# Step-size products of a hybrid S5/SSD layer: three-part split operands against full f32 in four column strips

## The chip, the cores and the metric

One core of a Trainium2 chip runs one layer of a streaming encoder in f32. The engines are PE (TensorE, matrix products; its weight loads are listed as PEld), DVE (VectorE), ACT (ScalarE), POOL (GpSimd) and SP (which issues DMAs). The metric is the device time of one execution in microseconds, lower is better. Before the change it was 1020.19 us, the median of three runs (1015.82 to 1021.0).

## The reference, cut to what matters

```python
hn   = rmsnorm(h, norm_w)                       # h = x: (1, 1024, 1024)
proj = hn @ w_in                                # (1024, 5136)
u_s5, z_s5, z_ssd, xBC, dt_raw = split(proj)    # dt_raw: the last 16 columns
...
dt = softplus(dt_raw + dt_bias)                 # step sizes, 16 heads
A  = -exp(A_log)
a_cs = cumsum(dt * A)                           # within chunks of 64 steps
y = ssd_chunked(xs, dt, A, Bm, Cm) + Dh * xs
```

The change concerns dt_raw, the product of the normalised input with the last 16 columns of w_in. The root of the mean square, which the norm divides by, is one number for each of the 1024 time steps, so it can be applied after the product.

## The kernel before, in words

The input is held transposed: eight tiles xt of 128 channels by 1024 steps, loaded by L677 and L686. The large products run in a split form: an operand is rounded to the format fp32r (hi) and the rest kept beside it (lo), and a product is hi x hi + lo x hi + hi x lo, each in one pass of PE (dense_k, L149 to L154; every call is 512 columns wide).

The first stage (L654 to L739) does the following for each of the eight input tiles k: ACT makes hi = norm_w x xt (L704; L679 for the first tile, in halves), DVE makes lo (L705, L680), ACT squares xt (L711) and DVE adds the squares into acc (L712). The weight of the step sizes, wd (128 x 8 x 16), is loaded by L697; wdr holds its hi part in 16 columns and the rest in 16 more (L698, L699). L715 then multiplies, for each tile, both column halves h and both parts i of the input with the 32 columns of wdr, and adds up over the eight tiles in two banks of PSUM, dps. So there are 32 products of 128 x 32 weights with 128 x 512 columns, and rows 0 to 15 and 16 to 31 of the result belong to the two parts of the weight.

Behind the loop, L718 copies the 32 rows of dps to dtR. rsqrt_bcast (L169 to L185) sums acc over the partitions with an f32 product with ones (L176, two calls of 512 columns), and ACT turns it into rstdB, one over the root, on all partitions. dt_scale (L483, on GpSimd) multiplies dtR with rstdB into dtF, and reorders. The first three tiles of u (L721 to L725) need hi and lo of the un-normalised input and are scaled afterwards; everything behind them uses the normalised tiles, for which DVE multiplies xt with rstdB (L729), ACT rounds (L731) and DVE takes the rest (L735).

dt_chain (L487) transposes dtF and adds up its parts with eight small products (L491) with the constant sel, whose rows repeat the 16 x 16 identity eight times; then it computes softplus and the sums over a chunk. It runs after the third tile of u.

In s5_weights stands a product that is used for comparison: L373 multiplies f32 weights of 128 x 32 with 128 columns, for q = 0 to 3 into rows 32q to 32q + 31 of one bank, with tile_position=(0, 32 * q), two of them for each q.

A planner sets the order of the instructions on each engine when the kernel is built: it simulates the engines and takes, of the instructions whose inputs are there in its plan, the one that stands first in the program. On the chip each engine follows that order and waits by semaphores. Where `in_line` is called, an order is written out by hand (L708 and L739). DMAs are all issued from SP, in one queue.

Of the kernel before, what the change touches and what calls it, by code (L numbers as in the profile page):

```python
# [8 lines left out]
F32 = mybir.dt.float32  # L9
# [4 lines left out]
P = 128  # L14
# [40 lines left out]
def hybrid_layer(ctx: ExitStack, tc: tile.TileContext, xT, pT, w_in, w_dt, w_glu, w_out, w_gate, w_ple,  # L55
# [426 lines left out]

    def dt_scale(dtF, raw):  # L483
        G.tensor_tensor(dtF.rearrange("p (k t c) -> p t k c", k=8, t=8), raw.rearrange("p (t k c) -> p t k c", t=8, k=8),
                        rstdB[:32].rearrange("p (t k c) -> p t k c", t=8, k=8), ALU.mult)

    def dt_chain(dtF):  # L487
        with tc.tile_pool(name="pt", bufs=1) as pt:
            tp = psa()
            for k in range(8):  # L490
                T.matmul(tp[:, 16 * k:16 * k + 16], dtF[:, k * P:(k + 1) * P], cs_("sel")[:32], start=True, stop=True)  # L491
            e_ = pt.tile([P, P], F32, tag="e_", name="e_")
            w_ = pt.tile([P, P], F32, tag="w_", name="w_")
            s2 = pt.tile([P, P], F32, tag="s2", name="s2")
            fd = dt2.rearrange("p k h -> p (k h)")
            V.tensor_tensor(dt2, tp[:, :P].rearrange("p (k h) -> p k h", k=8),
                            pr("dtb")[:, None, :].broadcast_to([P, 8, 16]), ALU.add)

            S.activation(e_, fd, AF.Abs)
            S.activation(e_, e_, AF.Exp, scale=-1.0)  # L500
            V.tensor_scalar(w_, e_, 2.0, None, ALU.add)
            V.reciprocal(w_, w_)
            V.tensor_tensor(e_, e_, w_, ALU.mult)
            V.tensor_tensor(s2, e_, e_, ALU.mult)
            V.tensor_scalar(w_, s2, 2.0 / 17, 2.0 / 15, ALU.mult, ALU.add)
            for d in (13, 11, 9, 7, 5, 3, 1):
                V.tensor_tensor(w_, w_, s2, ALU.mult)
                V.tensor_scalar(w_, w_, 2.0 / d, None, ALU.add)
            V.tensor_tensor(w_, w_, e_, ALU.mult)
            V.scalar_tensor_tensor(fd, fd, 0.0, w_, ALU.max, ALU.add)  # L510
            nA = pt.tile([P, 16], F32, tag="nA", name="nA")
            S.activation(nA, pr("alog"), AF.Exp)
            V.tensor_scalar(nA, nA, -1.0, None, ALU.mult)
            a_ = pt.tile([P, 8, 16], F32, tag="a_", name="a_")
            V.tensor_tensor(a_, dt2, nA[:, None, :].broadcast_to([P, 8, 16]), ALU.mult)
            fa = a_.rearrange("p k h -> p (k h)")
            cp = psa()
            rp = psa()
            T.matmul(cp[:, 0:P], cs_("triM"), fa, start=True, stop=True)
            T.matmul(cp[:, P:2 * P], cs_("sup"), fa, start=True, stop=True)  # L520
            T.matmul(cp[:, 2 * P:3 * P], ones, fa, start=True, stop=True)
            T.matmul(rp[:, 0:P], fa, cs_("triM"), start=True, stop=True)
            T.matmul(rp[:, P:2 * P], fa, cs_("tri0"), start=True, stop=True)
            rows = pt.tile([P, 2, P], F32, tag="rows", name="rows")
            V.tensor_copy(csM, cp[:, 0:P])
            S.activation(dtd.rearrange("p k h -> p (k h)"), cp[:, P:2 * P], AF.Exp)
            V.tensor_tensor(dtd, dtd, dt2, ALU.mult)
            S.activation(totE, cp[:, 2 * P:3 * P], AF.Exp)
            V.tensor_copy(rows[:, 0], rp[:, 0:P])
            S.activation(rows[:, 1], rp[:, P:2 * P], AF.Exp)  # L530
            dma(Rd.rearrange("a p c -> p a c"), rows)
# [117 lines left out]
    xhl = []  # L649
    es_t = ExitStack()  # L650
    dpool = es_t.enter_context(tc.tile_pool(name="dpool", bufs=1))
    dtF = dpool.tile([32, NT], F32, tag="dtF", name="dtF")
    pu = es_t.enter_context(tc.tile_pool(name="pu", bufs=2))
    with tc.tile_pool(name="p0", bufs=2) as p0:  # L654
        acc = p0.tile([P, NT], F32, tag="acc", name="acc", bufs=1)
        wd = p0.tile([P, 8, 16], F32, tag="wd", name="wd", bufs=1)
        wdr = p0.tile([P, 8, 32], F32R, tag="wdr", name="wdr", bufs=1)
        wt, xts = [], []
        pu_ps = [[psd(), psd()], [psd(), psd()]]
        dps = [psa(), psa()]  # L660
        pu_ps.append([psa(), psa()])

        zero = p0.tile([P, 512], mybir.dt.bfloat16, tag="zero", name="zero", bufs=1)
        V.memset(zero, 0.0)
        for _ in range(NWARM):
            T.matmul(dps[0], zero[:, 0:P], zero, start=True, stop=True)
        for k in range(KT):
            xt = p0.tile([P, NT], F32, tag="xt", name="xt", bufs=8)
            if k == 0:

                hi, lo = xslot(k, "x")
                raw = wpool.tile([P, NT], F32, tag="wraw", name="wraw")
                whi = wpool.tile([P, NT], F32R, tag="whi", name="whi")
                wlo = wpool.tile([P, NT], F32R, tag="wlo", name="wlo")
                line = []
                for h in range(2):
                    dma(hf(xt, h), hf(xT[k], h))  # L677
                    dma(hf(raw, h), hf(wsrc[0][0], h))
                    line.append(S.activation(hf(hi, h), hf(xt, h), AF.Copy, scale=pr("normw", k)))  # L679
                    V.scalar_tensor_tensor(hf(lo, h), hf(xt, h), pr("normw", k), hf(f(hi), h), ALU.mult, ALU.subtract)  # L680
                    line.append(S.activation(hf(whi, h), hf(raw, h), AF.Copy))
                    V.tensor_tensor(hf(wlo, h), hf(raw, h), hf(f(whi), h), ALU.subtract)
                wt.append((whi, wlo))
                wat[0] = 1
            else:
                dma(xt, xT[k])  # L686
            if k == 2:
                dma(cst_t, cst)
                V.tensor_copy(ones_r, ones)
            if k == 1 or k == 4:  # L690
                wp[0] = wpool if k < 2 else p0
                wfetch(1)
                wt.append(wq.pop(0))
                wp[0] = wpool
            if k == 0:

                dma(wd.rearrange("p k m -> p (k m)"), w_dt)  # L697
                V.tensor_copy(wdr[:, :, 0:16], wd)  # L698
                V.tensor_tensor(wdr[:, :, 16:32], wd, f(wdr)[:, :, 0:16], ALU.subtract)  # L699
            xts.append(xt)  # L700
            if k > 0:
                hi, lo = xslot(k, "x")
                nw = pr("normw", k)
                S.activation(hi, xt, AF.Copy, scale=nw)  # L704
                V.scalar_tensor_tensor(lo, xt, nw, f(hi), ALU.mult, ALU.subtract)  # L705
            xhl.append((hi, lo))
            if k == 0:
                in_line(line + [S.activation(acc, xt, AF.Square)])  # L708
            else:
                sq = p0.tile([P, NT], F32, tag="sq", name="sq")  # L710
                S.activation(sq, xt, AF.Square)  # L711
                V.tensor_tensor(acc, acc, sq, ALU.add)  # L712
            for h in range(2):
                for i in range(2):
                    T.matmul(dps[h][:32], wdr[:, k], hf(xhl[k][i], h), start=(k == 0 and i == 0), stop=(k == 7 and i == 1))  # L715
        dtR = p0.tile([32, NT], F32, tag="dtR", name="dtR", bufs=1)
        for h in range(2):
            S.copy(hf(dtR, h), dps[h][:32])  # L718
        rsqrt_bcast(rstdB, acc, 1.0 / NT)
        dt_scale(dtF, dtR)  # L720
        for k in range(KT):  # L721
            for m in range(2):
                dense_k(pu_ps[m], wt[m], xhl, k, KT, HALVES)
        for k in range(KT):
            dense_k(pu_ps[2], wt[2], xhl, k, KT, HALVES)  # L725

        xhl, line = [], []
        for k in range(KT):
            line.append(V.scalar_tensor_tensor(xts[k], xts[k], pr("normw", k), rstdB, ALU.mult, ALU.mult))  # L729
            hi, lo = xslot(k, "xn")  # L730
            S.activation(hi, xts[k], AF.Copy)  # L731
            xhl.append((hi, lo))
            if k % 2:
                for i in (k - 1, k):
                    line.append(V.tensor_tensor(xhl[i][1], xts[i], f(xhl[i][0]), ALU.subtract))  # L735
            if k == 1:
                us = [pu.tile([P, NT], F32, tag="u", name="u") for _ in range(2)]
                line += [V.tensor_tensor(js(hf(us[0], h)), sj(pu_ps[0][h]), sj(hf(rstdB, h)), ALU.mult) for h in range(2)]
        in_line(line)  # L739
# [266 lines left out]
```

## Time and profile before

| what | value |
|---|---|
| median of three runs | 1020.19 us |
| profiled execution | 1020.48 us |
| its span, first to last instruction | 1018.2 us |
| PE busy | 970.5 us (95%) |
| DVE busy | 612.4 us (60%) |
| ACT busy | 458.4 us (45%) |
| POOL busy | 248.9 us (24%) |
| mean granted clock of PE | 0.980 of full speed |

The profile is of one execution. Busy times count an engine from the start to the end of each instruction. A matmul lasts longer than the distance to the next, since they are pipelined: what one costs is read from the distance between two starts. An f32 product shows as more than one record with its weight load. An entry such as 128*32 128x512 is the weight's rows and columns, and the moving operand.

### The profile page before, as it was taken

Reading aid. Unit: us, or ns where it says so; the run is one execution under the profiler, and the core shown is the slowest. Engines: PE = TensorE matmul, PEld = TensorE weight load, DVE = VectorE, ACT = ScalarE, POOL = GpSimd, SP = SyncE. Lnnn points to the kernel's source line nnn. Section 1 sums busy time; section 2 is a strip of 40 time slices with the busy share of each in tenths; the row PEclk is TensorE's granted clock in tenths of the full one; section 3 lists DMA queues with packets and bytes.
Section 4 is the critical chain, followed back from the end, with each engine's and each line's share of the span. In section 5 each row is a group of like instructions: output and inputs, shape, how many; then the busy total and the mean of one; then the engine's idle time right before and its main releaser. Section 6 shows DMA issues by size and latency. Waiting matters only on the chain. (4 is left out here: it accounts for less than half of the span.)

```text
span 1018.2 us, 13114 instructions
## 1 busy us (share of the span) xinstructions
PE 970.5 (95%) x4992; PEld 812.0 (80%) x4992; DVE 612.4 (60%) x971; ACT 458.4 (45%) x603; POOL 248.9 (24%) x167
## 2 busy tenths in 40 slices
PE   8999999989999999999799989999999989999994
PEld 5778777778888888888678768888887668899994
DVE  7698798936998991000568556687542411544577
ACT  8354142255765434332376353484213731462363
POOL 0000000000000050101033864333323174332454
PEclk9999999998999999999799999999999989999998
DMA  7135778496341228889946744576324650011133
GB/s 293 41 90 163 210 233 262 133 244 174 102 145 63 83 104 249 230 258 192 342 141 214 257 121 139 173 238 206 88 83 128 187 181 30 1 54 56 57 137 123
DMA packets 136270, 158.56 MB, mean 156 GB/s; under 512 B 6288, under 2 KB 108688, under 8 KB 135184
## 3 DMA queue, kind: packets, MB, share of 16 engines
q1 hardware_dynamic: 136208, 157.74, 51.5%
q8 instruction: 39, 0.64, 0.3%
q14 instruction: 23, 0.19, 0.1%
HBM read 118.06 MB, written 39.65 MB: 155 GB/s over the span
## 5 line engine op out<-in xcount | busy, mean ns | idle before, releaser
L133 POOL TENSOR_TENSOR wlo<-wraw,whi 128x1024 fp32r<-128x1024 f32 x52 | 139.5, 2685 | 286.9 <-ACT whi L130 213.6
L130 ACT ACTIVATE whi<-wraw 128x1024 fp32r<-128x1024 f32 x79 | 83.3, 1055 | 260.2 <-PE psd L154 211.9
L154 PE MATMUL psd<-xnlo,whi 128*128 128x512 f32 x592 | 185.5, 393 | 0.2 <-DVE xnlo L735 0.2
L154 PE MATMUL psd<-xnhi,wlo 128*128 128x512 f32 x592 | 185.4, 393 | 0.2 <-DVE wlo L133 0.2
L154 PE MATMUL psd<-xnhi,whi 128*128 128x512 f32 x592 | 184.4, 392 | 0.0
L154 PEld LDWEIGHTS psd<-xnlo,whi 128*128 128x128 f32 x592 | 111.0, 188 | 24.6 <-DVE xnlo L735 1.0
L154 PEld LDWEIGHTS psd<-xnhi,wlo 128*128 128x128 f32 x592 | 110.8, 188 | 24.6 <-issue 1.6
L154 PEld LDWEIGHTS psd<-xnhi,whi 128*128 128x128 f32 x592 | 110.8, 188 | 23.4 <-issue 0.8
L566 DVE SCALAR_TENSOR_TENSOR csB<-csB,csM,cst_t 128x128 f32<-128x128 f32 x128 | 50.3, 466 | 119.5 <-DMA zc<-Zd 108.1
L546 DVE SCALAR_TENSOR_TENSOR cv<-pad,prm_t,cv 128x1024 f32<-128x1024 f32 x48 | 65.6, 1366 | 3.6 <-ACT cv L544 3.3
L154 PE MATMUL psd<-hhi,whi 128*128 128x384 f32 (+1 forms) x192 | 50.7, 318 | 0.5 <-DVE gt L875 0.5
L154 PE MATMUL psd<-hlo,whi 128*128 128x384 f32 (+1 forms) x192 | 50.8, 317 | 0.0
L154 PE MATMUL psd<-hhi,wlo 128*128 128x384 f32 (+1 forms) x192 | 50.7, 317 | 0.0
L154 PE MATMUL psd<-nhi,whi 128*128 128x512 f32 x128 | 41.1, 407 | 6.4 <-ACT whi L130 3.8
L133 DVE TENSOR_TENSOR wlo<-wraw,whi 128x1024 fp32r<-128x1024 f32 x27 | 32.8, 1219 | 23.1 <-PE psd L154 15.8
L849 DVE TENSOR_TENSOR h<-h,psd 128x512 f32<-128x512 f32 x16 | 10.3, 682 | 58.6 <-PE psd L154 58.6
L154 PE MATMUL psd<-yhi,whi 128*128 128x512 f32 x128 | 40.5, 396 | 4.3 <-DVE m L809 4.2
L537 POOL MEMSET pad<- 128x3 f32 x16 | 1.6, 102 | 175.5 <-DMA Cd<-pad 161.3
L154 PE MATMUL psd<-nlo,whi 128*128 128x512 f32 x128 | 41.5, 404 | 0.1
L154 PE MATMUL psd<-ylo,whi 128*128 128x512 f32 x128 | 41.4, 398 | 0.0
L154 PE MATMUL psd<-nhi,wlo 128*128 128x512 f32 x128 | 41.0, 404 | 0.0
L154 PE MATMUL psd<-yhi,wlo 128*128 128x512 f32 x128 | 40.8, 397 | 0.0
(291 smaller groups left out, 1894.3 us busy)
## 6 DMA issues: line engine op xcount, KB each, us to landing
wraw<-in_w_in_dram SPq DMA_DIRECT2D x39, 512.0 KB, 4.3
Cd<-pad SPq DMA_DIRECT2D x16, 512.0 KB, 2.9
Zd<-z SPq DMA_DIRECT2D x16, 512.0 KB, 5.9
ug<-Ud SPq DMA_DIRECT2D x16, 512.0 KB, 4.3
cc<-Cd SPq DMA_DIRECT2D x8, 1024.0 KB, 6.7
csB<-Rd SPq DMA_DIRECT2D x8, 1024.0 KB, 11.6
wraw<-in_w_out_dram SPq DMA_DIRECT2D x16, 512.0 KB, 3.4
wraw<-in_w_gate_dram SPq DMA_DIRECT2D x16, 512.0 KB, 3.4
```

Source lines behind the costliest of these rows:

```text
L130: S.activation(hi, raw, AF.Copy)
L133: E.tensor_tensor(lo, raw, f(hi), ALU.subtract)
L154: T.matmul(p, w[:, c], rhs[k][r][:, x], start=(k == 0 and j == 0), stop=(k == nk - 1 and j == 2))
L537: G.memset(pad[:, 8:11, 0:1], 0.0)
L546: conv_last[0] = V.scalar_tensor_tensor(cv, pad[:, d:d + 8, 1:129], pr("convw", 4 * m + d), cv, ALU.mult, ALU.add)
L566: i_ = V.scalar_tensor_tensor(csB[:, h], csB[:, h], csM[:, 16 * k + h:16 * k + h + 1], cap, ALU.subtract, ALU.min)
L849: V.tensor_tensor(hf(h_t[m], h), hf(h_t[m], h), ps[h], ALU.add)
```

## The change

wdr becomes f32: 128 x 8 x 32, with zeros in 16 of the 32 columns and norm_w x wd in the others. The products read the input tile xt itself instead of its hi and lo, without norm_w, which the weight now holds. They are issued at k = 3 and at k = 7 for four tiles each; tile k - 3 + q goes to rows 32q to 32q + 31 of dps, in the array's column strip q. So each strip adds up two tiles, dps has 128 rows, and dtR and dtF have 128 partitions instead of 32. dt_scale and L491 take 128 rows; sel, whose rows repeat, adds up the four strips.

```diff
     def dt_scale(dtF, raw):
         G.tensor_tensor(dtF.rearrange("p (k t c) -> p t k c", k=8, t=8), raw.rearrange("p (t k c) -> p t k c", t=8, k=8),
-                        rstdB[:32].rearrange("p (t k c) -> p t k c", t=8, k=8), ALU.mult)
+                        rstdB.rearrange("p (t k c) -> p t k c", t=8, k=8), ALU.mult)
...
-                T.matmul(tp[:, 16 * k:16 * k + 16], dtF[:, k * P:(k + 1) * P], cs_("sel")[:32], start=True, stop=True)
+                T.matmul(tp[:, 16 * k:16 * k + 16], dtF[:, k * P:(k + 1) * P], cs_("sel"), start=True, stop=True)
...
-    dtF = dpool.tile([32, NT], F32, tag="dtF", name="dtF")
+    dtF = dpool.tile([P, NT], F32, tag="dtF", name="dtF")
...
-        wdr = p0.tile([P, 8, 32], F32R, tag="wdr", name="wdr", bufs=1)
+        wdr = p0.tile([P, 8, 32], F32, tag="wdr", name="wdr", bufs=1)
...
-                V.tensor_copy(wdr[:, :, 0:16], wd)
-                V.tensor_tensor(wdr[:, :, 16:32], wd, f(wdr)[:, :, 0:16], ALU.subtract)
+                V.memset(wdr, 0.0)
+                V.tensor_tensor(wdr[:, :, 0:16], wd, pr("normw")[:, :, None].broadcast_to([P, 8, 16]), ALU.mult)
...
-            for h in range(2):
-                for i in range(2):
-                    T.matmul(dps[h][:32], wdr[:, k], hf(xhl[k][i], h), start=(k == 0 and i == 0), stop=(k == 7 and i == 1))
-        dtR = p0.tile([32, NT], F32, tag="dtR", name="dtR", bufs=1)
+            if k % 4 == 3:
+
+                for h in range(2):
+                    for q in range(4):
+                        T.matmul(dps[h][32 * q:32 * q + 32], wdr[:, k - 3 + q], hf(xts[k - 3 + q], h),
+                                 start=(k == 3), stop=(k == 7), tile_position=(0, 32 * q))
+        dtR = p0.tile([P, NT], F32, tag="dtR", name="dtR", bufs=1)
         for h in range(2):
-            S.copy(hf(dtR, h), dps[h][:32])
+            S.copy(hf(dtR, h), dps[h])
```

## Rows read from the trace of the kernel before

**Rows 1.** The page, part 1: busy us (share of the span) and instructions of each engine.

```profile
PE 970.5 (95%) x4992; PEld 812.0 (80%) x4992; DVE 612.4 (60%) x971; ACT 458.4 (45%) x603; POOL 248.9 (24%) x167
```

**Rows 2.** Stretch, length; busy us of PE, PEld, DVE, ACT, POOL; clock, DMA, GB/s.

```profile
5.00:10.00 5.00, 3.47 (x11) 1.40 (x10) 3.04 (x6) 3.82 (x6) 0.00 (x0) 1.00 0.99 356
10.00:15.00 5.00, 4.81 (x22) 3.27 (x21) 4.96 (x6) 4.79 (x6) 0.00 (x0) 1.00 1.02 417
...
20.00:25.00 5.00, 5.00 (x24) 3.51 (x23) 5.00 (x5) 4.95 (x6) 0.00 (x0) 1.00 0.31 120
```

**Rows 3.** Timeline of PE, 9 to 13 us: start us, us, engine, line, operation.

```profile
9.15 0.43 PE L715 MATMUL psa<-xhi,wdr 128*32 128x512 f32 x1 [0.20 <-DVE wdr L699]
...
10.10 0.62 PE L715 MATMUL psa<-xhi,wdr 128*32 128x512 f32 x2
...
11.38 0.65 PE L715 MATMUL psa<-xlo,wdr 128*32 128x512 f32 x2 [0.19 <-DVE xlo L705]
11.87 0.62 PE L154 MATMUL psd<-xlo,whi 128*128 128x512 f32 x2
12.33 0.63 PE L154 MATMUL psd<-xhi,wlo 128*128 128x512 f32 x2
```

**Rows 4.** Instructions of line L715: duration ns min/median/max, first and last start.

```profile
L715 PE MATMUL psa<-xhi,wdr x16: 387/396/426, 9.1 to 30.9; 128*32 128x512 f32 x16
```

**Rows 5.** Timeline of PEld (weight loads), 33 to 36 us.

```profile
33.67 0.41 PEld L176 LDWEIGHTS psa<-acc,cst_t 128*128 128x128 f32 x2
34.32 0.19 PEld L176 LDWEIGHTS psa<-acc,cst_t 128*128 128x128 f32 x1 [0.24 <-issue]
34.75 0.19 PEld L176 LDWEIGHTS psa<-acc,cst_t 128*128 128x128 f32 x1 [0.24 <-issue]
35.18 0.19 PEld L154 LDWEIGHTS psd<-xlo,whi 128*128 128x128 f32 x1 [0.24 <-issue]
```

**Rows 6.** Timeline of PE around L373, 109 to 112 us.

```profile
109.96 0.61 PE L154 MATMUL psd<-xnhi,wlo 128*128 128x512 f32 x2
110.50 0.66 PE L373 MATMUL psa<-CA,Bbd 128*32 128x128 f32 x14
111.09 0.73 PE L154 MATMUL psd<-xnhi,whi 128*128 128x512 f32 x2
111.66 0.39 PE L154 MATMUL psd<-xnlo,whi 128*128 128x512 f32 x1
```

**Rows 7.** Timeline of ACT and DVE, 14 and 27 us: one row each.

```profile
14.12 1.16 ACT L704 ACTIVATE xhi<-xt,prm_t 128x1024 fp32r<-128x1024 f32 x1 [0.21 <-DMA xt<-in_xT_dram]
...
27.64 1.22 DVE L712 TENSOR_TENSOR acc<-acc,sq 128x1024 f32<-128x1024 f32 x1
```

**Rows 8.** Timeline of DVE and PE, with line L484's own row between.

```profile
38.98 4.74 DVE L729 SCALAR_TENSOR_TENSOR xt<-xt,prm_t,rstdB 128x1024 f32<-128x1024 f32 x2 [10.12 <-ACT rstdB L185]
...
49.95 2.46 DVE L729 SCALAR_TENSOR_TENSOR xt<-xt,prm_t,rstdB 128x1024 f32<-128x1024 f32 x2
...
L484 POOL TENSOR_TENSOR dtF<-dtR,rstdB x1: 2409/2409/2409, 39.0 to 39.0; 32x1024 f32<-32x1024 f32 x1
...
50.25 1.95 PE L491 MATMUL psa<-cst_t,dtF 32*128 32x16 f32 x16
```

**Rows 9.** Waits, us in total, times, longest: 50 to 60 us, 60 to 230 us.

```profile
PEld psd L154 <- DVE xnlo L735: 0.8, 2, 0.6
...
PE psa L373 <- DVE CA L366: 2.6, 2, 1.3
PE psa L373 <- DVE CA L363: 0.9, 2, 0.6
...
PE psa L407 <- DMA ug<-Ud: 4.1, 1, 4.1
```

**Rows 10.** The page, part 5: line L133 on GpSimd, busy us, mean ns, idle before.

```profile
L133 POOL TENSOR_TENSOR wlo<-wraw,whi 128x1024 fp32r<-128x1024 f32 x52 | 139.5, 2685 | 286.9 <-ACT whi L130 213.6
```

**Rows 11.** Busy time by stretch again, 210 to 240 us.

```profile
210.00:240.00 30.00, 25.45 (x133) 22.14 (x132) 7.42 (x8) 16.21 (x29) 0.27 (x4) 0.89 0.93 224
```

## The prediction, made before the changed kernel was run

> **What bounds the kernel now.** I read the page's busy times first: PE (TensorE's matmuls) is busy 95% of the span, DVE 60% [rows 1]. So time taken from PE is time off the end, wherever PE has work queued. Next the busy times by stretch over the first 40 us, where the edited instructions lie [rows 2]: PE is short of work from 5 to 10 us (3.47 of 5 us), nearly full from 10 us (4.81 of 5), and full in 20 to 25 us, while the loads end soon after 20 us (DMA share 0.31 in 20 to 25 us, so some 1.6 us of it). Then PE's own order there, instruction by instruction [rows 3]: the step-size products of L715 stand between the dense ones of L154, two at a time, as each half of an input tile gets ready. PE's order is fixed when the kernel is built: a planner simulates the engines and issues what its plan holds ready, earlier program lines first. The pairs of L715 (the hi part for both column halves, later the lo part) show this, since the program's own loop would put hi and lo beside each other. Last I read what follows: the squares' sum [rows 5, 7], rstdB and the normalised tiles on DVE [rows 8], and the places where PE later waits for DVE [rows 9].
>
> **What is removed.** 32 products of 128x32 by 128x512 in one pass (16 on the hi part, row shown, 16 on the lo part alike) [rows 4]. In the full stretch two follow each other in 0.46 us (11.87 to 12.33) [rows 3], so each costs 0.23 us of PE although one lasts 0.396, and 32 cost 7.3 us. Not all of it is on the path. The first eight run from 9.15 to about 11.87, when PE has little else: after them it waits for xlo of the second tile, which comes at 11.38 [rows 3]. Without them the four dense products that start at 11.87 could start at 11.38: 0.5 us. The other 24 stand in the full stretch: 24 x 0.23 = 5.5 us. Saved: 6.0 us.
>
> **What is added.** 16 products in f32. How the chip runs f32 with 512 columns is shown by the squares' sum at L176: two calls make four records, whose weight loads start 0.43 us apart (34.32, 34.75, 35.18) [rows 5]. So one f32 product is two passes of 0.43 us, and 16 are 32 passes: 13.8 us if they run one by one. Whether four tiles in four column strips run at once is shown by L373, which has the same stationary shape (128x32, f32), the same four strips and 128 columns. There 14 passes take 0.66 us from first start to last end [rows 6]. A pass of 128 columns by the 0.43 us for 512 is 0.107 us, so 14 in a row would be 1.5 us plus the tail; four strips, of which the fullest has four passes, are 4 x 0.107 = 0.43 us plus a tail of some 0.25. The second fits. The same rows give the price of going in and out: the dense product before starts at 110.18 (second of the two at 109.96), the next would have started at 110.41 and starts at 111.09, and the two there take 0.57 instead of 0.46. That is 0.68 + 0.11 = 0.79 us for 0.43 us of streaming, so 0.36 us for one clump.
>
> One tile's pair (both column halves, two passes each) lies in one strip: 4 x 0.43 = 1.72 us, and 2.07 us with the way in and out. Pairs that stand together share those 2.07 us; pairs with dense products between them pay it each. Two whole groups of four are 4.1 us; eight lone pairs are 16.6.
>
> The TensorE page of the Trainium skill ("TensorE: Matmul & The Clock Gate", Part 3: Packing small matmuls) says that matmuls start and end strictly in program order. By that a strip's second pass would hold back the next strip's first, and L373's passes in its program's order would need about eleven rounds, or 1.2 us plus the tail. The 0.66 us speaks against it; the rule is a rival below.
>
> **How the passes will stand.** The new products read the input tiles themselves, so in the plan a pair is ready when its tile has landed, not when hi and lo are made. The tiles land over the first 21.6 us: the fourth at 14.1 us, for which ACT waits [rows 7], the last by about 21.6 [rows 2]. Between these two lie six loads of one size, four tiles and two of weights: some 1.25 us each, so tiles come 1.25 or, with a weight load between, 2.5 us apart, around the 1.72 us of a pair. So I expect neither one clump for each group nor eight lone pairs. Pairs one and two stand together before 10.4 us, in the gap that the first old products filled, and cost nothing; if that cover is gone they cost 2.07. Of the other six I take three clumps, of one, two and three pairs: 3 x 2.07 = 6.2 us. PE: 6.2 - 6.0 = +0.2 us. The bounds are -3.9 (one clump on the path) and +6.4 (six lone pairs, 12.4 - 6.0).
>
> **What moves with it.** PE gets to L176 at 33.67 [rows 5], but its input acc is ready at 27.64 + 1.22 = 28.86 [rows 7]: rstdB comes 4.8 us later than it could, because PE has a backlog ahead of L176. DVE's chain of the normalised tiles starts from rstdB, at 38.98 after a wait of 10.12 us [rows 8]. With more PE time given to the products, the plan puts fewer dense products ahead of L176, and rstdB can come 0 to 4.8 us earlier; I take half, 2.4 us, since the trace does not show the planner's price of an f32 pass. That is worth something as PE waits for DVE behind it: 0.8 us for xnlo at 50 to 60 us, and 2.6 + 0.9 us for CA at L373 from 60 to 230 us, 4.3 us together [rows 9]. Worth 2.4 us. A later acc cannot come of it: the sums on ACT and DVE are untouched.
>
> **The small edits.** The cast of wd and its remainder become a memset, needing no load, and one product, on DVE, which is busy for 3.04 of 5 us there [rows 2]: 0, and 0.5 us if it had no gap. The copies to dtR keep 512 columns on each partition and only get more partitions: 0, at a place where PE holds the queue ahead of rstdB anyway. dt_scale on GpSimd goes from 32 to 128 partitions with the same 1024 elements each: it takes 2.41 us now [rows 8], and a 128x1024 operation of GpSimd takes 2.69 [rows 10]. So 0 to +0.3 us; I take 0.1, near the row of the same operation. DVE does feel it: its two L729 beside dt_scale take 4.74 us, two others 2.46 [rows 8], and PE would see at most that 0.3. L491 has the weights 128 rows deep instead of 32, with 16 passes in 1.95 us as before [rows 8]: 0. No queue gets a new DMA.
>
> **The sum.** The profiled execution took 1020.48 us (span 1018.2 and 2.3 around it), 0.3 above the median of 1020.19. 1020.5 + 0.2 + 0.1 - 2.4 = 1018.4 us.
>
> **The rivals.**
> A, fours together: the planner holds a group as one clump, as L373's 14 are. PE: between 2.07 and 4.1 on the path, -3.9 to -1.9, say -2.9, and rstdB moves by a little more, -1: 1016.6. For it: [rows 6]. Against it: L373's inputs come at once, from one operation, the tiles do not.
> B, lone pairs (slower): dense products get between all six pairs; it decides as soon as tiles land further apart in the plan than a pair takes there. Each strip then works alone, 12.4 us against 6.0: +6.4, less up to 2.4 from rstdB: 1024.5 to 1027. For it: L715's halves stand apart, with dense work between them [rows 3].
> C, PE waits at L176: the plan overrates the passes, puts so few dense products ahead that PE arrives before 28.86, and waits in order. Ten dense products fewer are 2.3 us; some 40 fewer would be 9.2, against 4.8 of backlog: a wait of about 4.4 us. Around a PE wait of 4.1 us [rows 9] the granted clock of 30 us is 0.89 [rows 11]: 0.11 x 30 x 2 = 6.6 us at 1.2 instead of 2.4 GHz, so 3.3 us more lost. The early rstdB gives 4.3 back: +3.4, or 1024.0.
> D, strips in program order: a pair's last pass holds the next pair's first back, so the clumps take 4, 7 and 10 rounds of 0.43 us and three times 0.36, 10.1 instead of 6.2 us: 1022.3. [rows 6] speak against it. This is the Trainium skill's rule above.
> E, no strips at once: the change would not do what it says. Six pairs of 1.72 us and the first two in a row: +5.9, less up to 2.4: about 1026. Against it: [rows 6].
> F, the planner's order shifts far behind this stage, since its whole plan is made anew; a few us either way.
>
> **How the numbers follow.** Forecast 0.38, A 0.22, B 0.16, C 0.10, D 0.05, E 0.04, F 0.05. A measurement of this kernel can tell about 0.5%, or 5.1 us, from no change. The forecast, D and most of C are within that. Of A I count 0.08 as faster (its bound with all of rstdB's 4.8 us, 1015.5 or less, and the scatter), of B 0.10 and of C 0.02 as slower, E 0.04 as slower, F 0.02 on either side. Faster 0.10, same 0.72, slower 0.18. The range takes in A's better end and B's worse: 1013.5 to 1026.
>
> **What would show it.** In the changed trace: 32 passes of 128x32 f32 at the products' line, and their starts: four within a few tens of ns, rounds 0.43 us apart, where pairs stand together (right), rounds of one (B or E). The first L176 load between 29 and 33 us, with no PE wait of over 1 us before it (C if there is one). rstdB's wait on DVE shorter than 10.12 us, the waits for xnlo and CA under 4.3 us in sum. GpSimd's dt_scale at 2.4 to 2.7 us. The prediction is wrong if the passes in four strips take turns, or if the order behind 230 us changes by more than the early stage does.

## The result and the profile after

The changed kernel takes 1033.39 us (median of 4 runs, 1030.49 to 1035.9) where the kernel before took 1020.6 beside it: a ratio of 1.0102, 95% interval 1.0071 to 1.0133. It is slower by one per cent, outside the predicted range of 1013.5 to 1026 us. The ratios here and below are not worked out from the medians: these lie 12.8 us apart, while the ratio makes it 10.4 us. The profiled execution took 1034.04 us, with a span of 1031.8: 13.6 us more than that of before.

The page, part 1, answers to [rows 1]:

```profile
PE 974.6 (94%) x4992; PEld 808.2 (78%) x4992; DVE 615.7 (60%) x971; ACT 459.3 (45%) x604; POOL 245.6 (24%) x167
```

PE has 4.1 us more work than before. Its idle time, span less busy, went from 47.7 to 57.2 us. So about a third of the longer span is work and two thirds are waits. Where each lies is shown by the busy time by stretch (stretch, length, busy us of PE, PEld, DVE, ACT, POOL; clock, DMA share, GB/s). First before, then after, each in its own fence:

```profile
0.00:590.00 590.00, 566.62 (x2833) 461.91 (x2834) 390.07 (x617) 268.38 (x359) 82.83 (x76) 0.98 0.62 184
590.00:860.00 270.00, 259.23 (x1305) 212.38 (x1304) 132.49 (x233) 119.08 (x129) 106.73 (x57) 0.97 0.47 145
```

```profile
0.00:590.00 590.00, 566.45 (x2816) 455.03 (x2817) 383.31 (x614) 266.58 (x358) 79.93 (x75) 0.99 0.62 181
590.00:860.00 270.00, 249.92 (x1262) 204.14 (x1261) 141.28 (x234) 119.19 (x128) 98.61 (x54) 0.97 0.51 148
```

Up to 590 us PE is as busy as before, but gets through 17 instructions fewer (2816 for 2833). From 590 to 860 us, some 530 us behind the last edited instruction, it loses 9.3 us. The extra work is that of the products, in the first 60 us. PE's timeline (start us, us, engine, line, operation) around one of the new pairs answers to [rows 3]:

```profile
8.07 1.92 PE L717 MATMUL psa<-xt,wdr 128*32 128x512 f32 x8
...
11.11 0.62 PE L154 MATMUL psd<-xhi,wlo 128*128 128x512 f32 x2
11.66 1.90 PE L717 MATMUL psa<-xt,wdr 128*32 128x512 f32 x4
13.49 0.73 PE L154 MATMUL psd<-xhi,whi 128*128 128x512 f32 x2
```

The first two tiles' pairs ran at once, eight passes in the time of four. The third tile's pair stands alone: the next dense product would have started at 11.11 + 0.46 = 11.57 and starts at 13.49, and its own two take 0.11 longer, so the pair costs 2.03 us. All six later pairs stand so, the others from 17.34, 22.16, 26.76, 29.48 and 31.98 us on. The groups of the products' line and of GpSimd's dt_scale (duration ns min/median/max, first and last start) answer to [rows 4] and [rows 8]:

```profile
L717 PE MATMUL psa<-xt,wdr x32: 592/592/617, 8.1 to 33.3; 128*32 128x512 f32 x32
...
L484 POOL TENSOR_TENSOR dtF<-dtR,rstdB x1: 2402/2402/2402, 48.7 to 48.7; 128x1024 f32<-128x1024 f32 x1
```

What follows the products has moved. Timelines of PE, ACT and DVE, which answer to [rows 5, 8]:

```profile
42.12 1.88 PE L176 MATMUL psa<-acc,cst_t 128*128 128x512 f32 x4
...
41.64 1.06 ACT L130 ACTIVATE whi<-wraw 128x1024 fp32r<-128x1024 f32 x1 [7.13 <-PE psd L154]
...
47.54 1.06 ACT L185 ACTIVATE rstdB<-acc 128x1024 f32<-128x1024 f32 x1
...
48.63 4.72 DVE L732 SCALAR_TENSOR_TENSOR xt<-xt,prm_t,rstdB 128x1024 f32<-128x1024 f32 x2 [1.15 <-ACT rstdB L185]
...
55.68 1.85 PE L491 MATMUL psa<-cst_t,dtF 128*128 128x16 f32 x16
```

L176 starts at 42.12 us, not earlier than before but 8.2 us later, and rstdB 9.7 us later. The six pairs are only part of that. Most of the rest is shown by the busy time of L154 alone up to the start of L176, before and after: 92 dense products stand ahead of it instead of 80. And on ACT the plan has put two casts of weights (L130, at 41.64 and 45.17 us) ahead of rstdB, which starts 5.42 us behind L176 where it was 4.00 (33.89 to 37.89).

```profile
0.00:33.89 33.89, 21.21 (x80) 14.94 (x80) 1.00 0.58 220
```

```profile
0.00:42.12 42.12, 23.83 (x92) 16.52 (x92) 1.00 0.46 177
```

L491 starts 5.4 us later than before, and the first pass of L373 7.0 later (114.9 for 107.9). The waits that I had hoped to shorten [rows 9] are shorter, with no gain in the end: from 60 to 230 us PE waits 1.9 and 0.3 us for CA, and from 50 to 60 us it waits for nothing.

```profile
PE psa L373 <- DVE CA L366: 1.9, 1, 1.9
...
PE psa L373 <- DVE CA L363: 0.3, 1, 0.3
```

### The profile page after: what moved, and what is told of

Same layout as the page of the kernel before. It is cut to its first block, busy times and chain, and to the rows that moved or that the text cites. A ratio compares the mean times of both kernels' runs of the same rounds, so it can differ in the third digit from the quotient of the medians.

```text
span 1031.8 us, 13121 instructions
## 1 busy us (share of the span) xinstructions
PE 974.6 (94%) x4992; PEld 808.2 (78%) x4992; DVE 615.7 (60%) x971; ACT 459.3 (45%) x604; POOL 245.6 (24%) x167
## 4 chain that ended last, share of the span: by engine, by line
PE 66%; DMA 13%; DVE 12%; ACT 4%; issue 3%; POOL 1%; SPq 1%; DVEq 0%; ACTq 0%; POOLq 0%
PE psd L154 54%; DVE csB L566 3%; DMA csB<-Rd 2%; DMA m2raw<-Sd 2%; PE psa L154 2%; DMA Yd<-tp 1%; PE psa L717 1%; DMA br<-in_brow_dram 1%; PE psa L460 1%; DVE xt L732 1%; PE psa L461 1%; PE psa L595 1%; DVE h L899 1%; PE psa L603 1%; PE psa L407 1%
## 5 line engine op out<-in xcount | busy, mean ns | idle before, releaser
L133 POOL TENSOR_TENSOR wlo<-wraw,whi 128x1024 fp32r<-128x1024 f32 x52 | 138.5, 2666 | 294.8 <-ACT whi L130 255.1
L130 ACT ACTIVATE whi<-wraw 128x1024 fp32r<-128x1024 f32 x79 | 83.4, 1056 | 250.9 <-PE psd L154 199.8
L154 PE MATMUL psd<-xnhi,wlo 128*128 128x512 f32 x592 | 186.5, 394 | 0.8 <-DVE wlo L133 0.8
L154 PE MATMUL psd<-xnhi,whi 128*128 128x512 f32 x592 | 186.1, 394 | 0.2 <-ACT u L752 0.2
L154 PE MATMUL psd<-xnlo,whi 128*128 128x512 f32 x592 | 185.6, 393 | 0.0
L154 PEld LDWEIGHTS psd<-xnhi,wlo 128*128 128x128 f32 x592 | 111.1, 188 | 26.0 <-issue 2.2
L154 PEld LDWEIGHTS psd<-xnhi,whi 128*128 128x128 f32 x592 | 111.1, 188 | 25.2 <-issue 1.4
L154 PEld LDWEIGHTS psd<-xnlo,whi 128*128 128x128 f32 x592 | 111.4, 189 | 23.2 <-issue 0.4
L566 DVE SCALAR_TENSOR_TENSOR csB<-csB,csM,cst_t 128x128 f32<-128x128 f32 x128 | 51.2, 473 | 117.2 <-DMA csB<-Rd 117.2
L133 DVE TENSOR_TENSOR wlo<-wraw,whi 128x1024 fp32r<-128x1024 f32 x27 | 32.9, 1220 | 32.3 <-ACT whi L130 32.3
L154 PE MATMUL psd<-hhi,whi 128*128 128x384 f32 (+1 forms) x192 | 50.8, 318 | 0.5 <-DVE gt L878 0.5
L154 PE MATMUL psd<-hlo,whi 128*128 128x384 f32 (+1 forms) x192 | 50.9, 318 | 0.0
L154 PE MATMUL psd<-hhi,wlo 128*128 128x384 f32 (+1 forms) x192 | 50.7, 318 | 0.0
L154 PE MATMUL psd<-nhi,whi 128*128 128x512 f32 x128 | 40.7, 404 | 8.3 <-ACT whi L130 4.8
L154 PE MATMUL psd<-nlo,whi 128*128 128x512 f32 x128 | 41.6, 405 | 0.0
L154 PE MATMUL psd<-yhi,whi 128*128 128x512 f32 x128 | 41.3, 399 | 0.0
L154 PE MATMUL psd<-nhi,wlo 128*128 128x512 f32 x128 | 41.0, 404 | 0.0
L154 PE MATMUL psd<-yhi,wlo 128*128 128x512 f32 x128 | 40.9, 397 | 0.0
L154 PE MATMUL psd<-mhi,wlo 128*128 128x512 f32 x128 | 40.5, 392 | 0.0
```

Source lines behind the costliest of these rows:

```text
L130: S.activation(hi, raw, AF.Copy)
L133: E.tensor_tensor(lo, raw, f(hi), ALU.subtract)
L154: T.matmul(p, w[:, c], rhs[k][r][:, x], start=(k == 0 and j == 0), stop=(k == nk - 1 and j == 2))
L566: i_ = V.scalar_tensor_tensor(csB[:, h], csB[:, h], csM[:, 16 * k + h:16 * k + h + 1], cap, ALU.subtract, ALU.min)
```

## The experiments

Ten kernels were run, in three sets, each beside its own runs of the kernel before. Three causes had to be told apart: the products themselves, the places where they stand on PE, and the order of everything behind the first stage, which the planner makes anew for the changed program. To tell them apart, most kernels have their orders written out. At the end of the program a list for each engine ties every instruction to the one ahead of it, with no semaphore and no work added:

```diff
+    for e, text in PIN.items():
...
+        for a, b in zip(order, order[1:]):
+            tc.add_manual_dep(mine[b], mine[a].name, mybir.DependencyInfo(mybir.DependencyClass.NoSync, mybir.DependencyReason.DATA),
```

So math and order can be chosen apart. All runs in one table (us; L176 and L491 are their first starts in the profiled execution, the last column is PE's busy time from 590 to 860 us, which was 259.23 before and 249.92 after):

| run | median | before beside it | ratio (95% interval) | L176 | L491 | PE 590 to 860 |
|---|---|---|---|---|---|---|
| e1: new products, order of before | 1032.49 | 1022.89 | 1.0105 (1.0057 to 1.0153) | 44.1 | 57.6 | 257.19 |
| e2: old products, order of after | 1032.33 | 1022.89 | 1.0084 (1.0052 to 1.0115) | 37.0 | 53.4 | 252.23 |
| e3: fours together, order of before | 1024.22 | 1022.89 | 1.0016 (0.9989 to 1.0042) | 36.1 | 50.4 | 257.72 |
| e4: fours together, planner's order | 1025.26 | 1022.89 | 1.0019 (0.9987 to 1.0050) | 36.2 | 50.5 | 254.76 |
| e5: old products, L176 earlier | 1019.59 | 1022.89 | 0.9971 (0.9949 to 0.9992) | 29.8 | 50.7 | 256.80 |
| e6: two clumps, gap filled | 1020.68 | 1022.89 | 0.9977 (0.9950 to 1.0004) | 32.5 | 48.8 | 259.18 |
| e7: e3 with filler products | 1022.76 | 1022.89 | 1.0001 (0.9974 to 1.0028) | 34.6 | 48.9 | 258.30 |
| e8: e6 with six lone pairs | 1028.59 | 1022.89 | 1.0071 (1.0046 to 1.0095) | 40.4 | 56.8 | 258.40 |
| e9: after, one spot as in before | 1036.68 | 1024.43 | 1.0106 (1.0060 to 1.0151) | 43.9 | 57.5 | 248.79 |
| e10: e6 with L176 ahead of clump | 1020.73 | 1024.43 | 0.9964 (0.9937 to 0.9991) | 28.6 | 48.7 | 259.07 |

### Math and order exchanged (e1, e2)

e1 is the changed kernel with the order of before on every engine. Only PE's first stage was left to the planner, as its instructions differ. e2 is the kernel before with the order of after, PE's first stage again left to the planner.

> The changed kernel, with the order of DVE, ACT, GpSimd, the DMA queue, and of PE behind the first three tiles of u, written out as it is in the kernel before; only PE's order in the first stage is left to the planner. Theory O (the changed kernel loses 5.4 us in the first stage, and the other 8 us because the planner wrote another order for the rest): L491 starts at about 55.7 us as in the changed kernel, the sixth h of L822 stays about 5.5 us behind the kernel before, and the time is 1026 us (+5 to +6). Theory S (the later start itself sets off the later waits, whatever the order): 1033 us, with waits of over 5 us again between 590 and 720 us.

> The kernel before, with the order of all engines written out as in the changed kernel, but for PE's first stage, which is left to the planner. Theory O: nothing is lost in the first stage (L491 at about 50 us), and the order behind costs about 8 us: 1028 us. Theory S: 1020 us, as the start is not later.

Busy time by stretch, e1 and then e2:

```profile
590.00:860.00 270.00, 257.19 (x1298) 211.23 (x1297) 139.47 (x234) 116.79 (x126) 108.20 (x59) 0.97 0.50 153
```

```profile
590.00:860.00 270.00, 252.23 (x1278) 205.90 (x1277) 141.74 (x234) 119.55 (x128) 102.21 (x57) 0.97 0.50 150
```

The loss behind 590 us goes with the order, not with the products: e2 has not one new product and lacks 7.0 us of PE work there, e1 has all of them and lacks 2.0. Nor is it that everything starts later: e1 is further behind at L373 than after. e2 is slower than before by 0.84%. But e1 came out slower than I had expected (1026). With its DVE order of before, wdr was made late and PE waited 0.71 us for it at 9.06 us. rstdB came 10.1 us later than before, L491 7.4 and L373 10.6 later. From there to the end the distance to before stays within 8 to 11 us. So e1 measures a first stage worse than that of after. e2 has a loss of its own in the first stage too, a granted clock of 0.52 from 10 to 15 us, so it is not the order behind 590 us alone: at the last L407 (254.8 us before) it is 8.4 us behind, at the end of the span 12.5. For after these are 5.7 and 13.6.

### Where the products stand (e3, e4, e7)

In e3 and e4 the eight products of a group follow each other by hand, the latest tile first, so that a group starts only when its four tiles are there:

```diff
-                for h in range(2):
-                    for q in range(4):
-                        T.matmul(dps[h][32 * q:32 * q + 32], wdr[:, k - 3 + q], hf(xts[k - 3 + q], h),
-                                 start=(k == 3), stop=(k == 7), tile_position=(0, 32 * q))
+                in_line([T.matmul(dps[h][32 * q:32 * q + 32], wdr[:, k - 3 + q], hf(xts[k - 3 + q], h),
+                                  start=(k == 3), stop=(k == 7), tile_position=(0, 32 * q))
+                         for h in range(2) for q in (3, 2, 1, 0)])
```

e3 has the order of before besides; e4 has the planner's own.

> The changed kernel with each group of eight products written out in line, that of the last tile first, so that they stand together on PE; the rest in the order of the kernel before. If four strips run at once with 512 columns: each group takes 4 rounds of 0.43 us and 0.3 us of way in and out, about 2.0 us from the dense product before to the one behind, against seven times 2.0 now; L491 starts at about 47.5 us, 2.7 earlier than in the kernel before, and the time is 1018 us (-2 to -3.5 against the kernel before). If only two strips run at once, or passes go in program order: 3.5 to 4 us for each group, L491 at about 51, 1021 us. If strips take turns: 7 us for each group, L491 at 57.

> The same products in two clumps, with the order of everything else left to the planner. First stage as in the kernel with the order of before (L491 at about 47.5 us). Theory O: behind it the planner's new order makes a difference of its own, a few us either way, so 1010 to 1028 us, with the difference to the first stage's gain made behind 200 us. Theory S: 1018 us, the same as with the order of before.

PE's timeline of e3, around the first clump and around its first product of the second tile:

```profile
17.66 0.62 PE L154 MATMUL psd<-xhi,whi 128*128 128x512 f32 x2
18.21 1.92 PE L715 MATMUL psa<-xt,wdr 128*32 128x512 f32 x16
20.07 0.73 PE L154 MATMUL psd<-xlo,whi 128*128 128x512 f32 x2
...
9.86 1.22 PE L154 MATMUL psd<-xhi,whi 128*128 128x512 f32 x2 [2.00 <-ACT xhi L704]
```

Sixteen passes take the time of four: the four strips do run at once, and the way in and out is paid once. The clump costs 20.07 - (17.66 + 0.46) + 0.11 = 2.06 us. That takes some 8 us off the time of e1 by the medians. But with no products in the early gap PE waits 2.00 us for the second tile. Behind that wait the granted clock is half, 1.2 instead of 2.4 GHz (0.50 from 10 to 15 us, with 11 PE instructions where before had 22 [rows 2]). So L491 comes at 50.4 us and the median is 1024, where 47.5 and 1018 were expected:

```profile
10.00:15.00 5.00, 4.90 (x11) 3.41 (x12) 5.00 (x6) 5.00 (x6) 0.00 (x0) 0.50 1.03 416
```

e4 has the same 0.50 in that stretch and 9 PE instructions; its median lies 1.0 us above that of e3, with intervals that overlap nearly whole.

e7, from the next set, fills that gap with eight products on the zero tile, on which no result hangs, and makes wdr early:

```diff
+        for _ in range(8):
+            T.matmul(dps[0], zero[:, 0:P], zero, start=True, stop=True)
         for k in range(KT):
             xt = p0.tile([P, NT], F32, tag="xt", name="xt", bufs=8)
```

> The kernel with two clumps of eight products (four strips at once) and the order of the kernel before, and with eight more products of the zero tile, as those of L666, put between the sixth dense product and the first of tile 1, where PE had waited 2.0 us for xhi at 7.9 to 9.9 us and then ran at half clock until 16.0; wdr is made early on DVE. Nothing of the result hangs on them. Theory (the moved products left a hole in which TensorE fell to 1.2 GHz, and the ten dense products behind it took 0.43 instead of 0.23 us each): with the hole filled the clock stays at its full level, L491 comes at 47 to 48 us instead of 50.4, time 2 to 3 us under that of the run without filling (1024.2): 1021 to 1022. Rival (the half clock has another cause, or the stage waits for the tiles anyway): L491 at 50, time 1024.

The same stretch in e7:

```profile
10.00:15.00 5.00, 4.62 (x20) 3.17 (x19) 4.42 (x5) 5.00 (x6) 0.00 (x0) 1.00 1.02 415
```

The clock stays at 2.4 GHz and 20 products run where 11 ran. L491 comes 1.5 us earlier than in e3 (48.9; 47 to 48 were expected), and the median is 1.5 us lower. The two intervals overlap for the most part, so a gain in time is not shown; the clock and the earlier L491 are in the rows, of one execution each.

### One clump or six lone pairs, all else equal (e6, e8)

Both have the products and the early wdr of after and the order of before behind the first stage, and PE's first stage is written out too. Tiles 0 and 1 multiply in the early gap. The two kernels differ only in where the other six pairs stand among the same 80 dense products:

```diff
 L154 x6, L717 tiles 0 and 1
-L154 x74, L717 tiles 2 to 7 in four strips, L176
+L154 x8, L717 tile 2, L154 x16, L717 tile 3, L154 x14, L717 tile 4,
+L154 x14, L717 tile 5, L154 x12, L717 tile 6, L154 x10, L717 tile 7, L176
```

> The changed kernel's own products, with every engine's order written out: behind the first stage the order is that of the kernel before, the weights wdr are made as early on DVE as in the changed kernel, tiles 0 and 1 multiply in the early gap at 8 us (two strips at once, 1.72 us), and the other six tiles in one clump of eight rounds of 0.43 us once the last tile is there, three to four strips at once, directly ahead of the reduction L176. Theory (what cost the changed kernel its time is where the products stand and what the planner did with the order, not the products): the clump takes 3.44 us and 0.35 for way in and out, the early gap keeps full clock from 10 us on, the reduction begins at about 30.7, L491 at 47.5 to 48.5 instead of 50.25 before, no waits beyond those of before, time 1016.5 to 1019.5. Rival (the f32 products are themselves dearer than the old ones, or the earlier rstdB gives nothing): L491 at 50 or later, time 1021 to 1026.

> The same kernel and the same orders as the run with one clump of twelve products, but these twelve stand as six lone pairs (one tile, its two halves) at six places among the dense products, the last directly ahead of the reduction; the two early tiles stay in the gap. Theory (a lone pair costs about 2.03 us, since one strip of the array at a time leaves three idle and the way in and out costs 0.3 each time): six times 2.03 is 12.2 against 3.8 for the one clump, so L491 comes 8.4 us later than in that run, first L373 and the end 8 to 9 us later: some 1025 to 1028. Rival (another stall of the first stage hides it, as rstdB's wait or the tiles' arrival): under 4 us later.

PE's timelines, e6 and then e8:

```profile
28.37 0.61 PE L154 MATMUL psd<-xhi,whi 128*128 128x512 f32 x2
28.91 3.63 PE L717 MATMUL psa<-xt,wdr 128*32 128x512 f32 x24
32.47 1.98 PE L176 MATMUL psa<-acc,cst_t 128*128 128x512 f32 x4
...
48.84 1.85 PE L491 MATMUL psa<-cst_t,dtF 128*128 128x16 f32 x16
```

```profile
18.27 0.61 PE L154 MATMUL psd<-xlo,whi 128*128 128x512 f32 x2
18.82 1.90 PE L717 MATMUL psa<-xt,wdr 128*32 128x512 f32 x4
20.65 0.74 PE L154 MATMUL psd<-xhi,wlo 128*128 128x512 f32 x2
...
40.38 1.98 PE L176 MATMUL psa<-acc,cst_t 128*128 128x512 f32 x4
...
56.75 1.85 PE L491 MATMUL psa<-cst_t,dtF 128*128 128x16 f32 x16
```

The 24 passes take 3.64 us as one clump (28.83 to 32.47) and 2.04 us for each lone pair, 12.2 for six. That is 8.6 us more; L176 and L491 come 7.9 us later, and the medians, of 12 runs each on the same chip, lie 7.9 us apart, with intervals that do not touch. This part is settled: the places alone cost some 8 us. e6 came out above the 1016.5 to 1019.5 that I expected, and its L176 1.8 us later than expected. In both executions the second tile came later than in after (ACT starts on it at 9.82 and 8.99 us, there at 8.01), and the pairs in the gap took 2.98 and 2.84 us instead of 1.92. By itself e6 (ratio 0.9977) is not told apart from the kernel before, so no gain by the f32 products is shown.

### One spot behind the first stage (e9)

What PE waits for from 590 to 860 us, in after (us in total, times, longest):

```profile
PE psa L166 <- ACT nh L164: 7.5, 1, 7.5
PE psd L154 <- ACT whi L130: 4.8, 3, 3.3
PE psd L154 <- ACT nhi L215: 3.5, 1, 3.5
```

and in before:

```profile
PE psd L154 <- DVE m L809: 4.2, 1, 4.2
PE psd L154 <- ACT whi L130: 3.8, 3, 1.8
PE psd L154 <- ACT nhi L215: 2.6, 1, 2.6
```

The longest, 7.5 us for nh, looks as if one engine's order made it. ACT has the exponential L570 ahead of L164, and L570 waits for DVE's sixteen L566, which here stand behind L611:

```profile
593.40 1.06 ACT L612 ACTIVATE zc<-ys 128x1024 f32<-128x1024 f32 x1 [16.38 <-DVE ys L611]
...
604.92 1.91 ACT L570 ACTIVATE csB<-csB 128x2048 f32<-128x2048 f32 x1 [7.09 <-DVE csB L566]
606.74 0.61 ACT L164 ACTIVATE nh<-zc 128x512 fp32r<-128x512 f32 x1
```

e9 is the changed kernel with its own order on all engines, and this one spot as in before:

```diff
 DVE
-L611, L566 x16
+L566 x16, L611
 ACT
-L612, L130, L811 x2, L570, L164
+L570, L130, L811 x2, L612, L164
```

> The changed kernel with its own order on every engine written out, but for one spot, that of the second of the eight SSD chunks: on DVE the sixteen L566 (csB less csM) stand ahead of L611 (ys times zc) instead of behind it, and on ACT the exponential L570 stands ahead of L612 (the square of ys) and L164 instead of between them; both as in the kernel before. The first stage is untouched. Theory (what the planner's other order behind the first stage costs is waits such as this one: PE's 7.5 us at 607 for nh, which stands on ACT behind an exponential that itself waits for DVE's sixteen): the wait falls to the 4 us that the kernel before had there, PE's loss in the stretch 590 to 735 from 11.7 to about 8, and the time by 3 to 4 us, to 1029 to 1030.5. Rival (the wait only moves: another engine or a transfer was late there too): PE waits 7 us at that place for something else, time 1033.

ACT's timeline of e9:

```profile
602.05 1.24 ACT L811 ACTIVATE psd<-psd,prm_t 128x512 f32<-128x512 f32 x2
603.20 1.05 ACT L612 ACTIVATE zc<-ys 128x1024 f32<-128x1024 f32 x1
605.63 0.63 ACT L164 ACTIVATE nh<-zc 128x512 fp32r<-128x512 f32 x1 [1.37 <-POOL zc L615]
```

My expectation missed, and the rival held in the main. The exponential is done by 599.8 us, but nh comes at 605.6, and PE waits 8.2 us for it. L612 now stands behind a pair L811 that starts only at 602.05, and GpSimd's L615 hangs on L612. The time is that of after (ratio 1.0106), though this execution lost 1.8 us more up to L491, at a granted clock of 0.74 from 5 to 10 us and 0.92 from 10 to 15, with the same order there. So the late loss is not that one swap. What e9 leaves as in after is PE's order. PE's timelines, before and then e9:

```profile
600.61 1.10 PE L154 MATMUL psd<-yhi,whi 128*128 128x512 f32 x2 [4.21 <-DVE m L809]
...
604.37 0.63 PE L166 MATMUL psa<-nh,ones_r 128*128 128x512 f32 x1
```

```profile
606.31 0.79 PE L166 MATMUL psa<-nh,ones_r 128*128 128x512 f32 x1 [8.22 <-ACT nh L164]
```

Before, PE first waits 4.21 us for L809 and has nine dense products to do from there to L166, so it does not wait for nh, which ACT starts at 602.77. In e9 it has no such work left ahead of L166 from 598.1 us on, though nh is only 2.9 us later. The late loss belongs to the orders of the engines together, and no single instruction was shown to carry it.

### What an earlier rstdB is worth (e5, e10)

e5 is the kernel before with the last twenty dense products ahead of L176 put behind it. e10 is e6 with L176 ahead of the clump of six pairs, and on ACT the copies of dtR behind rstdB:

```diff
 e5
-L154 x20, L176
+L176, L154 x20
 e10
-L154 x74, L717 tiles 2 to 7, L176
+L154 x74, L176, L717 tiles 2 to 7
```

> The kernel before, with each engine's order written out as it was, but for one edit: the last twenty dense products (L154) that stood ahead of the reduction of acc (L176) stand behind it. The reduction should begin at about 29.3 us, when DVE's last sum of acc has come, instead of 33.89, and rstdB should be there at 33.3 instead of 37.9. No product is added or taken away. Theory (the time of rstdB is worth something in this stage, as one point of the prediction assumed): the products L491 and the first xn products come up to 4.5 us earlier only where PE had been waiting, so the waits of 0.8 us for xnlo and of 2.6 and 0.9 for CA shrink, first L373 at 104 to 106 us instead of 107.9, time 1016 to 1019. Rival (PE is what bounds the stage, and rstdB at 37.9 was early enough): L491 stays at 50.3, first L373 at 107.9, time 1020 to 1022.

> The kernel with two clumps and the early gap filled, with the reduction of acc (L176) ahead of the second clump instead of behind it, and on ACT the two copies of dtR (L721) behind the root and the reciprocal. Nothing else is changed. Theory (with PE no longer waiting elsewhere, the last thing that the first stage waits for is xnlo and CA, which hang on rstdB): the reduction begins at 28.8 us instead of 32.5, rstdB comes at 33.5 instead of 37.1, PE's waits of 0.6 us for xnlo and 1.0 for CA go, first L373 at 105 instead of 106.4, time 1 to 1.5 us less. Rival (no engine is late by rstdB any more): L491 and L373 where they were, time the same.

The group of L373 (the last numbers are its first and last start), for e5, e6 and e10:

```profile
L373 PE MATMUL psa<-CA,Bbd x128: 272/273/297, 107.2 to 204.9; 128*32 128x128 f32 x128
```

```profile
L373 PE MATMUL psa<-CA,Bbd x128: 272/273/297, 106.4 to 202.6; 128*32 128x128 f32 x128
```

```profile
L373 PE MATMUL psa<-CA,Bbd x128: 272/273/298, 105.1 to 200.5; 128*32 128x128 f32 x128
```

In e5 rstdB comes 3.2 us earlier and L373 starts 0.7 earlier, not the 2 to 4 that I expected. In e10 rstdB comes 4.5 us earlier than in e6 (32.6 for 37.1) and L373 1.3 earlier. So in the trace an earlier rstdB is worth less than a third of itself, since PE had dense work to do in any case. Both kernels come out faster than before by 0.3 to 0.4%. Their intervals leave out a ratio of 1, but most of each lies within the 0.5% that I count as the same. e10 and e6 can't be told apart by their times (0.9964 and 0.9977).

## Why the prediction was wrong, step by step

**The price of a pass: right.** 0.43 us a pass, two passes a product, four strips at once, 0.35 us for the way in and out: the clump of e3 costs 2.06 us (2.07 in the prediction), a lone pair 2.03 to 2.04. The eight passes of the first two tiles ran in the early gap in 1.92 us, as the forecast had it. Rivals D and E fall with the 16 passes of e3 in 1.92 us. Under the rule on program order that I cited from the Trainium skill ("TensorE: Matmul & The Clock Gate", Part 3) they would have needed, by an estimate from that rule, nine rounds of 0.43 us, each product's second pass holding back the next one's first; they needed four. (For the sixteen passes of L373, of which the trace shows fourteen, it would be thirteen rounds and not the eleven of the prediction, which changes nothing in the argument.) So the trace does not agree with that rule for the single passes of strips that work on different columns; for products taken as wholes no run here speaks against it.

**How the passes will stand: wrong.** This is the first step that failed. I took three clumps for the six later pairs, from the time between two tiles' landing. The plan put dense products between all of them: rival B, which I gave 0.16. The term of 6.2 us measures 6 x 2.03 = 12.2. Rival B's time of 1024.5 to 1027, 4 to 6.5 us over before, is close to what e8 shows for it alone, 5.7 us over before by the medians. The last pair stands at 31.98 us, some ten us behind the last landing, so the tiles were not what held the pairs apart. Why the plan spread them so can't be read from a trace.

**L176 and rstdB: wrong in sign, small in weight.** This is the second step that failed. I expected fewer dense products ahead of L176 and took 2.4 us as gain; there were twelve more. rstdB came 9.7 us later. An explanation would be that the plan counts the new passes as shorter than they are; no run tested that. The sum was wrong in the worth of it as well: rstdB 3.2 us earlier brought L373 forward by only 0.7 in e5. The waits of [rows 9] were no measure of what is to be gained there.

**The order behind the first stage: put at nothing in the sum.** This is the third step that failed. Rival F had 0.05 and "a few us either way". PE's idle time grew by 9.5 us, of which 9.3 lie between 590 and 860 us. With the order of before at most 2.4 of them are left, whatever the products (256.8 to 259.2 us of PE work there in e1, e3, e5 to e8 and e10; the lowest is e5, which has the old products). With the order of after they come back without the products (252.23 in e2). The planner's third order, in e4, lies between (254.76). In time the order's share is less sure: 9.4 us by the medians of e2, whose first stage has a loss of its own, and 3 to 7 us from after against e8, by their ratios or their medians. In the traces e2 loses 4.1 us behind the last L407, and after loses 7.9 there, on top of 5.7 ahead of it. The prediction had named this as what would make it wrong, but its sum has no term for it.

**The small edits: right.** GpSimd's dt_scale takes 2.40 us on 128 partitions, DVE's two operations beside it 4.72 (4.74 before [rows 8]). No wait stands ahead of L176, so rival C is out.

**Rival A, fours together.** e3 and e4 gave 1.3 and 2.4 us more than before, not 3.9 less. The prediction had named the price of the lost cover, 2.07 us; that wait came (2.00 us), and half a clock came with it, which I had weighed only for rival C. With the gap filled, e7, which is otherwise this rival, comes to the time of before (ratio 1.0001). e6 and e10, with the cover kept and the other six pairs in one clump, come to 2.2 and 3.7 us less by the medians, of which only that of e10 is clear of no change.

## What to carry to other kernels

A saving in passes counts only where the passes stand together: here the same 24 passes cost 3.6 us in one place and 12.2 in six, so write the order of such products by hand rather than leave it to a planner. When a planner orders the whole program, an edit in the first 50 us is an edit of everything behind it. Exchange math and order in two runs before any cause is sought in the edited lines. And before a small job is taken out of a gap, ask what else the engine would do there: the wait is one price, the granted clock behind it another.

## What the runs showed of the hardware

Two things I had not expected. In e3 a single PE wait of 2.00 us, up to 9.86 us, was followed by a granted clock of 0.50 for the whole of 10 to 15 us; in e7, with eight products of the zero tile in its place, the clock was 1.00. But single executions differ: in e2 the clock was 0.52 there, with waits of 1.13 and 0.53 us before 8.6 us, and in e9, with a wait of 1.58 us up to 6.5, it was 0.74 from 5 to 10 us, where after, with the same order and 0.78 us of waiting, had 1.00. And DVE's L611 took 3.40 us in after, beside GpSimd's L808, and 1.21 in e9, where GpSimd had nothing to do. In after it starts 0.08 us behind L808, and its end, 593.32, is 1.09 us behind L808's end at 592.23, so it looks held until L808 is done:

```profile
589.92 3.40 DVE L611 TENSOR_TENSOR ys<-ys,zc 128x1024 f32<-128x1024 f32 x1 [5.89 <-POOL ys L607]
...
589.84 2.39 POOL L808 TENSOR_TENSOR m<-m,z 128x1024 f32<-128x1024 f32 x1
```

```profile
596.44 1.21 DVE L611 TENSOR_TENSOR ys<-ys,zc 128x1024 f32<-128x1024 f32 x1
```

This agrees with what the Trainium skill's page "SBUF — State Buffer" (section "SBUF: two separate sides") says of the pair of ports that DVE and GpSimd share, for a DVE instruction with two inputs in SBUF and a GpSimd one that reads SBUF: whichever starts first holds it for its whole instruction, and the other waits. So a changed order on GpSimd also changes how long DVE's instructions last.
